# Weight halves off the second vector engine, and both input halves in one 512-column product, in a two-block transformer kernel

## The chip, the cores and the metric

One core of one Trainium2 chip runs the whole kernel in one launch. The metric is the device time of the launch in microseconds. Its engines are named as in the profile: PE (TensorE, matrix products; PEld is its weight loads), DVE (VectorE), ACT (ScalarE), POOL (GpSimd) and SP (SyncE, which here only issues the weight transfers). Each engine runs its own instructions in the order in which they were placed and waits on semaphores for the others.

## The reference

256 tokens of width 1024 go through two blocks, all in fp32. Cut to its skeleton:

```python
# block 1, layer 0 with MLA attention, layer 1 with NSA attention
x = layer_norm(a*x + 0.5*swiglu(x, ffn_w_gu[l,0], ffn_w_down[l,0]), ...)
x = layer_norm(a*x + concat(attention(x), memory_attention(...)) @ w_out[l], ...)
x = layer_norm(a*x + 0.5*swiglu(x, ffn_w_gu[l,1], ffn_w_down[l,1]), ...)

def swiglu(x, w_gu, w_down):              # w_gu 1024 x 5632, w_down 2816 x 1024
    g, u = split(x @ w_gu, 2)
    return (silu(g) * u) @ w_down

# block 2, layer 0: HGRN2 mixer, layer 1: RG-LRU mixer, each followed by PEER
h = rms_norm(x) * (1 + sc1) + sh1;  x = x + g1 * mixer(h)
h = rms_norm(x) * (1 + sc2) + sh2;  x = x + g2 * peer_ffn(h)

def peer_ffn(h, w_q, sub_keys, u_tab, v_tab):    # 16384 experts, 16 of them per head and token
    scores of 8 heads x 2 halves x 128 keys; top 16 of each half      # "first level"
    top 16 of the 16 x 16 sums: ids; gate = softmax(top_s)            # "second level"
    act = gelu(u_tab[ids] . h);  out = sum(gate * act * v_tab[ids])

# RG-LRU, one direction
r, ig = sigmoid(block_diag(xc, w_a) + b_a), sigmoid(block_diag(xc, w_x) + b_x)
log_a = -8 * r * softplus(-lam);  a = exp(log_a)
hs = linear scan of (a, sqrt(-expm1(2*log_a)) * ig * xc)
```

The vector of modulations (sc, sh, g) comes from a product of the condition with a large matrix ("ada"), which the kernel spreads over earlier stages.

## The kernel before, in words

**Split weights.** PE multiplies fp32 in a rounded form (fp32r). So each operand is kept as two halves, `hi` (rounded) and `lo` (what rounding left), and each product is taken three times: x_hi by w_hi, x_lo by w_hi, x_hi by w_lo. The weights come from memory as tiles of 128 x 1024 fp32 (512 KB each, one SP transfer, `wload`). `split` (L256) makes `hi` by an ACT copy (L262) and `lo` by a subtraction (L263). `lo_engine` (L247) says where the subtraction runs: `lo_pat` is a string cycled through, "V" for DVE and "P" for POOL. It is "VP" by default, so every second one is POOL's; after a norm the next `calm` (4 or 2) go to POOL whatever the pattern says. HGRN uses "PPV", the LRU "VPP" and "P", and the expert stages "V". `hi_pat` does the same for `hi` between ACT and DVE.

**linear** (L307) takes a weight tile of eight 128 x 128 pieces and streams the 256 tokens past it in three passes of eight products, 256 columns each: hi with XH, hi with XL, lo with XH. XH and XL are the two halves of the stage's input, two tiles. The feed-forward layers (`ffn`, L458) have 22 steps j, each of two tiles (gate and up) into the two halves of one PSUM bank, then a silu on ACT (L481), a multiply on DVE (L482) and the split of the result into AH and AL; then eight `down` products of 22 pieces each, with a residual sum. `stream(4, 3)` gives six places for a `hi` and its `lo`, so splits run some five tiles ahead. In each of 96 places one "fill" of the ada product runs on DVE (L966, L967). The first products after a norm (`begin`, `raws`) run on values that are not yet normalised.

**hgrn** (L1135) builds, per pair of heads, decayed queries and keys with many 128 x 256 DVE products (L1254, where one of the key products is POOL's). **lru** (L1446) has the gate loop (L1484 on: sigmoid, a DVE scaling at L1507, a tanh, a POOL product at L1510), an exponential (L1526), and scans (L1542). **peer** (L1565) multiplies by 16 wq tiles while DVE finds each first level (L1592 to L1596), and then takes 128 u tiles (`u_tile`) beside a list `todo` of smaller steps: 16 second levels, decodes, turns and gates. In the loop a `budget` grows by 1.7 a tile and a step is placed when the budget holds its cost. v tiles follow (`accumulate_tokens`, products of 512 columns at L1405 to L1407).

**What sets the order.** The order of each engine's instructions is fixed when the program is built, by a scheduler of the tile framework that goes by data dependences, the order in the code and a cost model. The pools limit how far a step may run ahead. PSUM has eight banks, four "mm" (matrix results of `linear`) and four "ax".

## Time and profile before

| | |
|---|---|
| median of 3 runs | 3166.89 us (3162.74 to 3168.49) |
| profiled execution | 3169.3 us, its span 3167.5 us |
| mean granted TensorE clock | 0.976 of full speed |
| PE busy | 3023.3 us, 95% of the span |
| DVE busy | 2360.8 us, 75% |
| ACT busy | 1656.8 us, 52% |
| POOL busy | 814.0 us, 26%, all but a little of it before 1412 us and between 2160 and 2400 us |

The stages, in us of the span: feed-forward 0 to 205, MLA to 350, feed-forward to 540 and (after a norm) to 765, NSA to 905, feed-forward to 1110, HGRN 1130 to 1345, expert searches to 1412, u tiles to 1800, v tiles to 2160, LRU to 2335, the second expert stage to the end. The rows are read as follows. "Busy" of PE includes time in which its pipeline is filled by overlapping products, so its pace is better read from the starts of successive groups of products. The mean duration of one instruction of a group, beside that of the same instruction at its fastest, shows whether it was held up while it ran. The chain of waits, followed back from the end, says which engine's work the end hung on.

### The profile page before, as it was taken

The page shows a single profiled execution, that of the slowest core. Times are in us where ns is not written, and L with a number is a line of the kernel's source. Part 1 is how long each engine was busy: PE and PEld are TensorE (multiplying, and loading weights), DVE is VectorE, ACT ScalarE, POOL GpSimd, SP SyncE. Part 2 cuts the span into 40 slices and gives each one's busy share as a digit, 9 for nine tenths or more (in the row PEclk, how much of TensorE's full clock was granted, in tenths as well). Part 3 has the DMA queues.
Part 4 walks back from the last instruction along what each step waited for, and adds up shares of the span by engine and source line. Part 5 has one row for each costly group of instructions (what it writes and reads, how often), then busy time and mean ns, then how long its engine had stood idle before and what let it go on. Part 6 is the DMA issues. An engine that isn't in the chain of part 4 may idle for free.

```text
span 3167.5 us, 57343 instructions
## 1 busy us (share of the span) xinstructions
PE 3023.3 (95%) x22268; PEld 2831.5 (89%) x22268; DVE 2360.8 (75%) x4441; ACT 1656.8 (52%) x2879; POOL 814.0 (26%) x393
## 2 busy tenths in 40 slices
PE   9999999999989979889999999998788999999998
PEld 8997999999789969889999988887788999988887
DVE  6866976964588598699888755558989888855555
ACT  5546554655554456546554555555545555455554
POOL 5643554755235345420000000003640000000000
PEclk9999999999999989999999999999899999999999
DMA  7852685885148433346444566665345544556664
GB/s 275 288 182 87 223 284 187 285 272 172 32 159 293 165 113 121 107 141 185 153 152 152 166 193 195 194 194 168 94 127 154 173 154 154 154 183 195 194 193 140
DMA packets 155794, 558.39 MB, mean 176 GB/s; under 512 B 17409, under 2 KB 19201, under 8 KB 155265
## 3 DMA queue, kind: packets, MB, share of 16 engines
q1 hardware_dynamic: 155232, 554.19, 54.1%
q8 instruction: 175, 2.87, 0.4%
q14 instruction: 99, 0.80, 0.1%
q10 hardware_dynamic: 288, 0.52, 0.0%
HBM read 553.60 MB, written 1.05 MB: 175 GB/s over the span
## 4 chain that ended last, share of the span: by engine, by line
PE 80%; DVE 14%; ACT 3%; issue 2%; DMA 1%; POOL 0%; DVEq 0%; ACTq 0%; SPq 0%; POOLq 0%
PE ps_mm L324 46%; PE ps_ax L1406 7%; PE ps_ax L1405 7%; PE ps_ax L1407 7%; PE ps_mm L1729 3%; DVE lo L263 2%; PE ps_mm L649 1%; PE ps_ax L324 1%; ACT hi L262 1%; DVE X L1051 1%; DVE RS L1113 1%; DVE M L1594 1%; PE ps_ax L540 1%; DVE M L1593 1%; DVE M L1596 1%
## 5 line engine op out<-in xcount | busy, mean ns | idle before, releaser
L262 ACT ACTIVATE hi<-raw 128x1024 fp32r<-128x1024 f32 (+1 forms) x948 | 987.4, 1048 | 868.8 <-PE ps_mm L324 382.8
L263 DVE TENSOR_TENSOR lo<-raw,hi 128x1024 fp32r<-128x1024 f32 (+2 forms) x698 | 919.6, 1319 | 530.7 <-ACT hi L262 519.3
L263 POOL TENSOR_TENSOR lo<-raw,hi 128x1024 fp32r<-128x1024 f32 (+2 forms) x261 | 663.7, 2549 | 1378.7 <-ACT hi L262 1326.8
L324 PE MATMUL ps_mm<-XH,hi 128*128 128x256 f32 (+1 forms) x4056 | 616.4, 290 | 26.8 <-ACT XH L1059 11.8
L324 PE MATMUL ps_mm<-XH,lo 128*128 128x256 f32 (+1 forms) x4056 | 587.5, 286 | 22.4 <-DVE lo L263 21.7
L324 PE MATMUL ps_mm<-XL,hi 128*128 128x256 f32 (+1 forms) x4056 | 585.1, 285 | 8.6 <-DVE XL L1060 5.6
L324 PEld LDWEIGHTS ps_mm<-XH,hi 128*128 128x128 f32 x4056 | 539.3, 192 | 35.4 <-ACT XH L1059 14.2
L324 PEld LDWEIGHTS ps_mm<-XH,lo 128*128 128x128 f32 x4056 | 535.2, 193 | 24.0 <-DVE lo L263 23.2
L324 PEld LDWEIGHTS ps_mm<-XL,hi 128*128 128x128 f32 x4056 | 532.0, 192 | 11.2 <-DVE XL L1060 7.7
L1407 PE MATMUL ps_ax<-lo,ah 128*128 128x512 f32 x1024 | 398.3, 389 | 0.0
L1406 PE MATMUL ps_ax<-hi,al 128*128 128x512 f32 x1024 | 398.3, 389 | 0.0
L1405 PE MATMUL ps_ax<-hi,ah 128*128 128x512 f32 x1024 | 398.3, 389 | 0.0
L1405 PEld LDWEIGHTS ps_ax<-hi,ah 128*128 128x128 f32 x1024 | 192.2, 188 | 40.1
L1407 PEld LDWEIGHTS ps_ax<-lo,ah 128*128 128x128 f32 x1024 | 192.2, 188 | 39.8
L1406 PEld LDWEIGHTS ps_ax<-hi,al 128*128 128x128 f32 x1024 | 192.2, 188 | 39.6
L1123 POOL TENSOR_SCALAR X<-X,VEC 128x256 f32<-128x256 f32 x4 | 3.7, 922 | 788.8 <-ACT RS L1109 786.8
L967 DVE SCALAR_TENSOR_TENSOR raw<-raw,one,cb 128x1024 f32<-128x1024 f32 x96 | 180.4, 1879 | 3.1 <-DMA raw<-in_ada_dram 0.2
L1736 ACT ACTIVATE M<-ps_mm 128x368 f32<-128x368 f32 (+42 forms) x128 | 43.8, 342 | 181.7 <-DVE M L1734 181.7
L1723 DVE TENSOR_TENSOR oh<-first,W 128x768 bf16<-128x768 bf16 x256 | 130.7, 550 | 0.0
L1729 PE MATMUL ps_mm<-oh 128*128 128x128 bf16 x1536 | 111.1, 220 | 0.0
L263 DVE TENSOR_TENSOR al<-M,ah 128x256 fp32r<-128x256 f32 x256 | 106.7, 418 | 1.2 <-ACT ah L262 1.2
L262 ACT ACTIVATE AH<-act 128x256 fp32r<-128x256 f32 x88 | 36.5, 417 | 133.4 <-DVE act L482 124.8
(457 smaller groups left out, 4044.2 us busy)
## 6 DMA issues: line engine op xcount, KB each, us to landing
raw<-in_pu_dram SPq DMA_DIRECT2D x256, 512.0 KB, 3.6
raw<-in_pv_dram SPq DMA_DIRECT2D x256, 512.0 KB, 3.5
raw<-in_gu_dram SPq DMA_DIRECT2D x175, 512.0 KB, 4.7
raw<-in_ada_dram SPq DMA_DIRECT2D x96, 512.0 KB, 4.5
raw<-in_down_dram SPq DMA_DIRECT2D x64, 512.0 KB, 4.4
raw<-in_hgin_dram SPq DMA_DIRECT2D x32, 512.0 KB, 3.6
raw<-in_wq_dram SPq DMA_DIRECT2D x32, 512.0 KB, 3.6
raw<-in_down_dram SPq DMA_DIRECT2D x32, 384.0 KB, 3.9
```

Of the source, the lines that this page charges most:

```text
L262: self.nc.scalar.activation(hi, src, AF.Copy)
L263: (eng or self.lo_engine()).tensor_tensor(lo, src, hi, op=ALU.subtract)
L324: mm(out, w[a][:, k], xin[b][:, k0 + k], start=k0 == 0 and at == 0, stop=k0 + n == kt and at == 3 * n - 1)
L540: nc.tensor.transpose(pt[:, bs], P[:, bs], self.ident)
L649: m(self.acc[b][:, k * T:k * T + T], w[:, 2 * b + k], x, start=t == 0 and w is hi and x is xh and k == 0, stop=t == KT - 1 and w is lo and ...
L967: nc.vector.scalar_tensor_tensor(w, w, tick, cb, op0=ALU.mult, op1=ALU.mult, accum_out=self.MOD[:, l, j:j + 1])
L1405: m(o, xh[:, ts], hi[:, cs], start=t == 0, stop=False)
L1406: m(o, xl[:, ts], hi[:, cs], start=False, stop=False)
L1407: m(o, xh[:, ts], lo[:, cs], start=False, stop=t == n - 1)
L1723: nc.vector.tensor_tensor(oh[:, q, 1:], first[:, q, None].to_broadcast([128, 3, 128, 2]), W3[:, :, None, t0 + 2 * q:t0 + 2 * q + 2].to_bro ...
L1729: nc.tensor.matmul(p[:, at:at + 128], oh[:, q, 0, :, t], oh[:, q, 1 + n, :, t], start=n == 0, stop=n == 2)
L1736: nc.scalar.activation(M[:, n:, ts], pv[:, n:], AF.Copy)
```

## The change

1. **lo.** `lo_pat` becomes "V" everywhere and `calm` goes. POOL keeps the subtraction only in `peer`: for most wq tiles, which a pattern "P" set inside `peer` (L1611) gives it before and now, and for u tiles that are placed while the next step of `todo` is a second level. There the budget grows by 2.4 a tile and a second level costs 2.4 (before 1.7 and 2.0), so one is placed per tile.
2. **Wide products.** XH and XL become the two halves of one tile XX, AH and AL of one tile AHL. `linear_wide` streams both at once: one product of 512 columns per piece of hi (x_hi into the bank's left half, x_lo into the right), then one of 256 columns per piece of lo into the left half. `fold` then adds the right half to the left: an ACT copy out of PSUM (L328) and a DVE add (L329). The feed-forward layers use it for gate and up, except for the first products after a norm, and for all `down` products. Each of gate and up now takes a bank of its own.
3. **HGRN** makes its last key product (28 instructions) on DVE. **LRU**: `hi` from "VA" and "V" to "A" and "VA"; the scaling at L1507 (16 instructions) is dropped, since tanh and exp now take a scale per channel, so that each of them runs 16 times on 256 columns where it ran 8 times on 512; the product at L1510 (8 instructions) goes from POOL to DVE.

```diff
@@ lo_engine
-        if self.calm:
-            self.calm -= 1
-            return self.nc.gpsimd
         e = self.lo_pat[self.lo_n % len(self.lo_pat)]
@@ new
+    def fold(self, p, t):
+        self.nc.scalar.activation(t, p[:, T:], AF.Copy)
+        self.nc.vector.tensor_tensor(p[:, :T], p[:, :T], t, op=ALU.add)
+
+    def linear_wide(self, p, wsrc, kt, xin, chunk=8):
+        mm = self.nc.tensor.matmul
+        for k0 in range(0, kt, chunk):
+            n = min(chunk, kt - k0)
+            hi, lo = self.first or self.wsplit(wsrc[:, k0:k0 + n, :], (n, 128))
+            self.first = None
+            for k in range(n):
+                mm(p.rearrange("p (a t) -> p a t", a=2), hi[:, k], xin[:, k0 + k], start=k0 + k == 0, stop=False,
+                   skip_group_check=True)
+            for k in range(n):
+                mm(p[:, :T], lo[:, k], xin[:, k0 + k, 0], start=False, stop=k0 + k == kt - 1, skip_group_check=True)
@@ ffn
+                        p = [self.ps(), self.ps()]
+                        for s in range(2):
+                            self.linear_wide(p[s], gu[li, j, s], KT, self.X2)
+                            self.fold(p[s], (sg, act)[s])
+                        nc.scalar.activation(sg, p[0][:, :T], AF.Silu)
+                        nc.vector.scalar_tensor_tensor(act, sg, 0.5, p[1][:, :T], op0=ALU.mult, op1=ALU.mult)
...
-                    self.linear(p[:, :T], self.A["down"][li, k], NF, (AH, AL))
+                    self.linear_wide(p, self.A["down"][li, k], NF, AHL)
+                    self.fold(p, pool.tile([128, T], F32, name="sg"))
@@ hgrn, lru
-                            (K[:, 1], K[:, 1], 1, eb[1][:, :, 0:1], nc.gpsimd)):
+                            (K[:, 1], K[:, 1], 1, eb[1][:, :, 0:1], nc.vector)):
...
-                                nc.vector.tensor_scalar(R[:, d, k], R[:, d, k], w[:, 4, c:c + 1], None, op0=ALU.mult)
+                                nc.scalar.activation(HS[:, d, k], R[:, d, k], AF.Tanh, scale=w[:, 4, c:c + 1])
-                    nc.scalar.activation(HS[:, d, k2], R[:, d, k2], AF.Tanh)
-                    nc.gpsimd.tensor_tensor(IG[:, d, k2], IG[:, d, k2], xc[:, k2], op=ALU.mult)
+                    nc.vector.tensor_tensor(IG[:, d, k2], IG[:, d, k2], xc[:, k2], op=ALU.mult)
@@ peer
-            second = [[(2.0, lambda h=h, a=a: second_level(h, a)) for h in range(8)] for a in range(2)]
+            second = [[(2.4, lambda h=h, a=a: second_level(h, a), "P") for h in range(8)] for a in range(2)]
...
-                budget += 1.7
+                side = todo[0][2:] if todo else ()
+                self.lo_pat = side[0] if side else "V"
+                budget += 2.4 if side else 1.7
```

What stands on the engines before and after, at three places (line numbers of the changed kernel are some 2 to 25 higher). **DVE in the first feed-forward layer's steps j**, before, two steps (`raw_…`, `cb` and `one` are the ada fill; every second step has the two `lo`):

```order
L482 SCALAR_TENSOR_TENSOR act_1387<-sg_1386,ps_mm_1388 128x256
L966 TENSOR_SCALAR one_1455<-act_1387 128x1
L967 SCALAR_TENSOR_TENSOR raw_1453,MOD_71<-raw_1453,one_1455,cb_614 128x1024
L263 TENSOR_TENSOR AL_145<-act_1387,AH_144 128x256
L482 SCALAR_TENSOR_TENSOR act_1459<-sg_1458,ps_mm_1460 128x256
L966 TENSOR_SCALAR one_1527<-act_1459 128x1
L967 SCALAR_TENSOR_TENSOR raw_1525,MOD_71<-raw_1525,one_1527,cb_614 128x1024
L263 TENSOR_TENSOR lo_1744<-raw_1741,hi_1743 128x1024
L263 TENSOR_TENSOR lo_1786<-raw_1783,hi_1785 128x1024
```

and now, one step:

```order
L329 TENSOR_TENSOR ps_mm_963<-ps_mm_963,sg_961 128x256
L260 TENSOR_TENSOR lo_1155<-raw_1152,hi_1154 128x1024
L260 TENSOR_TENSOR lo_1179<-raw_1176,hi_1178 128x1024
L329 TENSOR_TENSOR ps_mm_964<-ps_mm_964,act_962 128x256
L504 SCALAR_TENSOR_TENSOR act_962<-sg_961,ps_mm_964 128x256
L990 TENSOR_SCALAR one_1019<-act_962 128x1
L991 SCALAR_TENSOR_TENSOR raw_1017,MOD_70<-raw_1017,one_1019,cb_546 128x1024
L260 TENSOR_TENSOR AHL_143<-act_962,AHL_143 128x256
```

Each step has both its `lo` and both folds on DVE; the `lo` placed there belong to tiles some six ahead of the fold. **PE at the same place**, before, one step of two tiles:

```order
L324 MATMUL ps_mm_691<-XH_68,hi_694 128x256 x8
L324 MATMUL ps_mm_691<-XL_69,hi_694 128x256 x8
L324 MATMUL ps_mm_691<-XH_68,lo_695 128x256 x8
L324 MATMUL ps_mm_691<-XH_68,hi_724 128x256 x8
L324 MATMUL ps_mm_691<-XL_69,hi_724 128x256 x8
L324 MATMUL ps_mm_691<-XH_68,lo_725 128x256 x8
```

and now, a step and the beginning of the next:

```order
L340 MATMUL ps_mm_963<-XX_68,hi_967 128x512 x8
L343 MATMUL ps_mm_963<-XX_68,lo_968 128x256 x8
L340 MATMUL ps_mm_964<-XX_68,hi_991 128x512 x8
L343 MATMUL ps_mm_964<-XX_68,lo_992 128x256 x8
L340 MATMUL ps_mm_1024<-XX_68,hi_1028 128x512 x8
L343 MATMUL ps_mm_1024<-XX_68,lo_1029 128x256 x8
```

Two passes over the same hi have become one. **DVE at the start of the u tiles of the first expert stage** (first levels end at L1595 and L1596; L1629 to L1637 are second levels), before, with the `lo` of the first five u tiles:

```order
L263 TENSOR_TENSOR lo_16031<-raw_16028,hi_16030 128x1024
L1595 MAX M_15235<-M_15235 128x8
L263 TENSOR_TENSOR lo_16069<-raw_16066,hi_16068 128x1024
L1596 MAX_INDEX M_15235<-M_15235 128x8
L263 TENSOR_TENSOR lo_16107<-raw_16104,hi_16106 128x1024
L1637 MAX_INDEX M_15235<-M_15235 128x8
L1629 TENSOR_TENSOR M_15235<-M_15235 128x256 x2
L1633 MAX M_15235<-M_15235 128x8 x2
L1634 MAX_INDEX M_15235<-M_15235 128x8
L263 TENSOR_TENSOR lo_16145<-raw_16142,hi_16144 128x1024
L1635 MATCH_REPLACE M_15235<-M_15235 128x256
L263 TENSOR_TENSOR lo_16183<-raw_16180,hi_16182 128x1024
```

and now, around the first `lo` of a u tile that DVE has there, that of tile 9 (the first levels end some forty rows ahead of the first row):

```order
L1706 TENSOR_REDUCE gst_14541<-M_13783 128x8
L1661 MAX M_13783<-M_13783 128x8
L1707 RECIPROCAL gst_14541<-gst_14541 128x8
L1662 MAX_INDEX M_13783<-M_13783 128x8
L1708 TENSOR_TENSOR M_13783<-M_13783,gst_14541 128x128
L1698 TENSOR_TENSOR M_13783<-M_13783 128x2048
L1654 TENSOR_TENSOR M_13783<-M_13783 128x256
L1700 TENSOR_TENSOR M_13783<-M_13783 128x2048
L1658 MAX M_13783<-M_13783 128x8
L260 TENSOR_TENSOR lo_14892<-raw_14889,hi_14891 128x1024
L1702 TENSOR_TENSOR M_13783<-M_13783 128x8x128
L1659 MAX_INDEX M_13783<-M_13783 128x8
```

The `lo` of tiles 0 to 8 are POOL's now; that of tile 9 stands on DVE behind seven second levels and ten decode instructions.

## Rows read from the trace of the kernel before

**Rows 1.** The page: busy time by engine; the chain of waits by engine.

```profile
PE 3023.3 (95%) x22268; PEld 2831.5 (89%) x22268; DVE 2360.8 (75%) x4441; ACT 1656.8 (52%) x2879; POOL 814.0 (26%) x393
...
PE 80%; DVE 14%; ACT 3%; issue 2%; DMA 1%; POOL 0%; DVEq 0%; ACTq 0%; SPq 0%; POOLq 0%
```

**Rows 2.** Stretches: width, busy us (count) of PE, PEld, DVE, ACT, POOL; clock.

```profile
13.00:121.00 108.00, 107.83 (x892) 107.75 (x892) 86.17 (x112) 60.66 (x87) 65.99 (x29) 0.98 0.81 280
...
205.00:350.00 145.00, 134.70 (x938) 119.33 (x937) 104.63 (x242) 94.62 (x204) 53.45 (x27) 0.98 0.35 120
...
1130.00:1345.00 215.00, 192.78 (x1413) 183.27 (x1413) 171.06 (x293) 130.47 (x272) 111.18 (x66) 0.94 0.35 111
...
2160.00:2260.00 100.00, 82.97 (x592) 80.49 (x591) 95.60 (x134) 59.91 (x109) 61.33 (x30) 0.88 0.44 147
2260.00:2335.00 75.00, 49.17 (x330) 46.60 (x329) 67.89 (x107) 29.78 (x56) 32.63 (x13) 0.82 0.27 86
```

**Rows 3.** Timeline of PE, feed-forward: start us, us, products (x8 a pass).

```profile
100.67 1.12 PE L324 MATMUL ps_mm<-XH,hi 128*128 128x256 f32 x8
...
110.21 1.12 PE L324 MATMUL ps_mm<-XL,hi 128*128 128x256 f32 x8
```

**Rows 4.** Timeline of PE, v tiles of the first expert stage, 512 columns.

```profile
1812.17 0.39 PE L1405 MATMUL ps_ax<-hi,ah 128*128 128x512 f32 x1
...
1818.29 0.39 PE L1405 MATMUL ps_ax<-hi,ah 128*128 128x512 f32 x1
```

**Rows 5.** Groups of DVE, 1500 to 1780 us (POOL idle): busy us, mean ns.

```profile
L263 DVE TENSOR_TENSOR lo<-raw,hi 128x1024 fp32r<-128x1024 f32 x81 | 99.2, 1225 | 35.7 <-ACT hi L262 32.7 <-ACT M L1744 1.7
```

**Rows 6.** Groups, feed-forward, 13 to 121 us, DVE and ACT.

```profile
L482 DVE SCALAR_TENSOR_TENSOR act<-sg,ps_mm 128x256 f32<-128x256 f32 x17 | 7.0, 411 | 0.1
...
L481 ACT ACTIVATE sg<-ps_mm 128x256 f32<-128x256 f32 x18 | 6.6, 366 | 0.0
```

**Rows 7.** DVE by line, whole span: ns of one, min/median/max.

```profile
L1051 DVE SCALAR_TENSOR_TENSOR X<-X,VEC,RS x24: 470/472/2642, 336.6 to 916.5; 128x256 f32<-128x256 f32 x24
...
L967 DVE SCALAR_TENSOR_TENSOR raw<-raw,one,cb x96: 1272/1289/3422, 66.7 to 1057.0; 128x1024 f32<-128x1024 f32 x96
...
L1254 DVE TENSOR_TENSOR Q<-Q,E x48: 400/416/2612, 1152.6 to 1275.8; 128x256 f32<-128x256 f32 x48
...
L1507 DVE TENSOR_SCALAR R<-R,spw x16: 334/581/2459, 2206.8 to 2238.6; 128x256 f32<-128x256 f32 x16
```

**Rows 8.** DVE group of L1051, whole span: busy us, mean ns.

```profile
L1051 DVE SCALAR_TENSOR_TENSOR X<-X,VEC,RS 128x256 f32<-128x256 f32 x24 | 22.9, 1022 | 0.0
```

**Rows 9.** MLA, 205 to 350 us: chain of waits by line, then DVE lo.

```profile
by line: PE ps_mm L649 12.5%; DVE lo L263 8.2%; ACT hi L262 5.9%; DVE X L1051 5.1%; PE ps_ax L776 5.1%; issue 4.5%; PE ps_ax L769 4.5%; PE ps_ax L540 3.9%; DVE RS L381 3.6%; DVE qt L670 3.2%; PE ps_ax L410 2.7%; ACT XH L447 2.3%; PE ps_ax L
...
L263 DVE TENSOR_TENSOR lo<-raw,hi 128x1024 fp32r<-128x1024 f32 x11 | 20.3, 1843 | 3.5 <-ACT hi L262 3.3
```

**Rows 10.** HGRN, 1130 to 1345 us: groups of DVE and of POOL.

```profile
L1254 DVE TENSOR_TENSOR Q<-Q,E 128x256 f32<-128x256 f32 x48 | 30.0, 654 | 0.0
...
L263 POOL TENSOR_TENSOR lo<-raw,hi 128x1024 fp32r<-128x1024 f32 x32 | 81.7, 2557 | 69.7 <-ACT hi L262 67.0 <-PE ps_mm L324 1.6 <-DVE K L1254 1.1
```

**Rows 11.** LRU, 2160 to 2335 us: groups of DVE and of POOL.

```profile
L263 DVE TENSOR_TENSOR lo<-raw,hi 128x1024 fp32r<-128x1024 f32 x9 | 21.2, 2359 | 1.3 <-ACT hi L262 1.1
...
L1507 DVE TENSOR_SCALAR R<-R,spw 128x256 f32<-128x256 f32 x16 | 14.3, 927 | 1.2 <-ACT R L1502 1.2
...
L263 POOL TENSOR_TENSOR lo<-raw,hi 128x1024 fp32r<-128x1024 f32 x29 | 74.6, 2585 | 67.1 <-ACT hi L262 50.7 <-issue 4.6 <-ACT late L1463 4.0
```

**Rows 12.** Timeline of PE at the first u tiles of both expert stages.

```profile
1384.62 1.11 PE L324 MATMUL ps_mm<-XH,hi 128*128 128x256 f32 x8
...
1400.78 5.49 PE L324 MATMUL ps_mm<-XH,lo 128*128 128x256 f32 x24 [10.26 <-DVE lo L263]
...
2391.09 5.43 PE L324 MATMUL ps_mm<-XH,lo 128*128 128x256 f32 x24 [8.03 <-DVE lo L263]
```

**Rows 13.** Groups of DVE, 1412 to 1500 us, POOL idle.

```profile
L1634 DVE FIND_INDEX8 M<-M 128x8 uint32<-128x256 f32 x10 | 4.2, 420 | 0.0
```

More of the change, by code (lines that the diff above doesn't have):

```diff
@@ L184, in __init__ @@
         self.seq_n = {"raw": 0, "hi": 0}
-        self.lo_pat = "VP"
+        self.lo_pat = "V"
         self.fills = deque()
@@ L189, in __init__ @@
         self.shift = None
-        self.calm = 0
         self.raws = deque()
@@ L207, in input_tiles @@
     def input_tiles(self):
-        self.XHc, self.XLc = (self.cp.tile([128, KT, T + 2], F32R, name=n, tag=n) for n in ("XH", "XL"))
+        self.XX = self.cp.tile([128, KT, 2, T + 2], F32R, name="XX", tag="XX")
+        self.XHc, self.XLc = self.XX[:, :, 0], self.XX[:, :, 1]
         self.XH, self.XL = self.XHc[:, :, :T], self.XLc[:, :, :T]
+        self.X2 = self.XX[:, :, :, :T]
     def constants(self, phases, bp):
@@ L442, in layer_norm @@
         self.fresh = True
-        self.calm = 4
         for k in range(KT):
@@ L461, in ffn @@
         with self.stream(4, 3), tc.tile_pool(name="ffn", bufs=2) as pool:
-            AH = pool.tile([128, NF, T], F32R, name="AH", bufs=1)
-            AL = pool.tile([128, NF, T], F32R, name="AL", bufs=1)
+            AHL = pool.tile([128, NF, 2, T], F32R, name="AHL", bufs=1)
+            AH, AL = AHL[:, :, 0], AHL[:, :, 1]
             gu = self.A["gu"]
@@ L622, in mix_start @@
         self.ob = self.ps("ax", 3)
-        self.zp = [self.cp.tile([128, 4, 512], F32, name=n, tag=t) for n, t in (("z", "XH"), ("P", "XL"))]
+        zp = self.cp.tile([128, 2 * KT * (T + 2)], F32, name="zp", tag="XX")
+        self.zp = [zp[:, 2048 * i:2048 * i + 2048].rearrange("p (a b) -> p a b", b=512) for i in range(2)]
         self.count = {"score": 0, "mixed": 0, "out": 0, "softmax": 0}
@@ L1027, in begin @@
         self.fresh = "banks"
-        self.calm = 2
         for n, src in enumerate(srcs):
@@ L1319, in hgrn @@
             self.rms_sum(pool)
-            self.lo_pat = "VP"
+            self.lo_pat = "V"
     def prepare(self):
@@ L1341, in prepare @@
         lam = self.vec("lru_lam_2", 0, 16)
-        w = self.sp = self.cp.tile([128, 5, 16], F32, name="spw")
+        w = self.sp = self.cp.tile([128, 6, 16], F32, name="spw")
         nc.scalar.activation(w[:, 0], lam, AF.Abs)
@@ L1486, in lru @@
                 if b:
-                    self.hi_pat = "VA"
-                    self.lo_pat = "VPP"
+                    self.hi_pat = "A"
+                    self.lo_pat = "V"
                 for d in range(2):
@@ L1513, in lru @@
             YB = pool.tile([128, KT], F32, name="YB")
-            self.hi_pat = "V"
-            self.lo_pat = "VPP"
+            self.hi_pat = "VA"
+            self.lo_pat = "V"
             self.hi_n = self.lo_n = 0
@@ L1525, in lru @@
                 for d in range(2):
-                    nc.scalar.activation(R[:, d, ks], R[:, d, ks], AF.Exp, scale=-2.0, bias=late[:, 0:1])
+                    for k in (2 * i, 2 * i + 1):
+                        nc.scalar.activation(R[:, d, k], R[:, d, k], AF.Exp, scale=w[:, 5, 8 * d + k:8 * d + k + 1],
+                                             bias=late[:, 0:1])
                     nc.vector.scalar_tensor_tensor(IG[:, d, ks], R[:, d, ks], 1.0, IG[:, d, ks],
@@ L1550, in lru @@
             self.hi_pat = "A"
-            self.lo_pat = "P"
+            self.lo_pat = "V"
             self.sqrt_soon(pool, Y[:, KT - 1, 0:1])
@@ L1562, in lru @@
             self.rms_sum(pool)
-            self.lo_pat = "VP"
+            self.lo_pat = "V"
     def peer(self, l):
@@ L1787, in peer @@
                 self.rms_sum(vpool)
-            self.lo_pat = "VP"
+            self.lo_pat = "V"
     def final(self):
```

9 lines of the change are left out of this document (5 added, 4 removed).

## The prediction

> **What bounds the kernel now.** I read the page first. PE is busy 95% of the span, DVE 75%, POOL 26%, and the chain of waits lies 80% on PE and 14% on DVE [rows 1]. That is an average over stages with different limits, so next the busy time by stretch. In the feed-forward layers (13 to 121 us) PE is busy 107.8 of 108 us: there only PE's pace counts, and DVE has 22 us of room. In MLA, HGRN and LRU PE has gaps, and in the LRU DVE is busy 163.5 of 175 us [rows 2]: there DVE's time counts.
>
> Third, how long a DVE instruction takes. The same L1051 instruction takes 0.470 us at its fastest and 2.642 at its slowest, and L1254, L967 and L1507 spread as widely [rows 7]. A `lo` on DVE takes 1.225 us where POOL is idle [rows 5], 1.843 in MLA [rows 9] and 2.359 in the LRU [rows 11], while POOL has `lo` of its own of about 2.57 us [rows 10, 11]. The slowest times are about a free instruction and most of one POOL instruction: DVE waits inside the instruction for POOL. So the change has three effects: a better PE pace in the feed-forward layers, freed DVE time elsewhere, and more work on DVE, namely POOL's.
>
> **Wide products.** Ten passes of eight 256-column products span 9.54 us, 119.3 ns each [rows 3]; 27 products of 512 columns span 6.12 us, 226.7 ns each [rows 4]. One wide product for two narrow ones saves 238.5 - 226.7 = 11.8 ns. The order has 152 wide tiles of gate and up (8 products each) and 32 `down` sums (22 each): 1216 + 704 = 1920, all in stretches that PE bounds. Term: **-22.7 us**.
>
> The Trainium skill ("TensorE: Matmul & The Clock Gate", "Back-to-back issue gap") gives an isolated warm product N/2.4 ns plus about 2.5, so a pair would save only those 2.5 ns, 4.8 us in all as an estimate. The trace's 119.3 ns for 256 columns is above its 109, and its 226.7 above its 216, so the rows decide.
>
> The price is a fold per tile. Its ACT copy is like L481 (0.366 us), its DVE add, with one operand in PSUM, like L482 (0.411, not slowed beside POOL) [rows 6]. A step j has 16 wide and 16 narrow products, 16 x (226.7 + 119.3) = 5.53 us of PE. DVE has in it two `lo` (2.45), two adds (0.82), L482 (0.41), AL (about 0.41, as L1254's 128 x 256 product) and, in most steps, a fill (1.27): 5.37 us, some 0.3 less where records overlap. That leaves hardly 5% but is below PE's time, and `lo` run some six tiles ahead, so a late fold delays nobody at once. I cost steady state at nothing; the cover is thin, and the first rival is its loss. At the end of each layer the last fold lies on the path: 0.37 + 0.41 = 0.8 us, four times. Term: **+3.2**.
>
> **Norms and transitions around the feed-forward layers.** L1051 takes 24 x (1.022 - 0.470) = 13 us more than at its fastest [rows 7, 8], at the head of MLA and in two transitions. Summing mean less fastest over the DVE pieces on the chain in the transitions between 350 and 1130 us gives about 25 us in all. Against it, some ten `lo` there (the `calm` ones) now stand on DVE in front of or between these, 10 x 1.225 = 12. Term: **-13**, between -25 and +3 (every `lo` exposed at both its own cost and a wait).
>
> **MLA.** Of the 145 us the chain has 8.2% on DVE `lo` (11.9 us), 5.1% on L1051 (7.4) and 3.2% on L670 (4.6) [rows 9]. At free durations these would be 11.9 x 1.225/1.843 = 7.9, 8 x 0.47 = 3.8 and (for three of L670's, of L1051's kind) 3 x 0.47 = 1.4: 10.8 us less, and the smaller pieces bring it to about 16. Eighteen `lo` come to DVE, 22 us, of which the chain's share of DVE's time (about 40 of 105 us) is 8. Term: **-8**. NSA has little POOL contention on its chain: **+1**.
>
> **HGRN.** The 48 L1254 products cost 48 x (0.654 - 0.400) = 12.2 us over their fastest [rows 7, 10]; the same over all DVE groups of the stage gives some 53. To DVE come 32 `lo` (39 us), 28 key products (11.5) and 6 small splits (2.5): 53. So DVE's 171 us [rows 2] stay. What changes is the chain, which has DVE on it for about 67 us: 22 of the excess lie on it and 6 of POOL's key products, and 53 x 67/171 = 21 come back. Term: **-7**, between -25 (all new `lo` beside other work) and +20 (half of them ahead of what PE waits for).
>
> **LRU.** Here DVE is full. Removed: 9 x (2.359 - 1.225) = 10.2 us on its `lo`, L1507's whole 14.3 us [rows 11], and about 42 of excess on some ten other kinds by the same rule, less 15 that stay because the next stage's wq `lo` remain on POOL; some seven `hi` casts that go to ACT, 4. Together 55. Added: 20 `lo` (29 on POOL less the wq ones [rows 11]), 24.5; eight products from POOL, about 0.68 each, 5.4; small splits, 2. Together 32. Net -23, of which DVE's 163.5/175 counts, and ACT's sixteen small exps for eight large ones cost a little: **-19**, between -30 and -5.
>
> **Expert stages.** PE stands 10.3 us at 1390.5 and 8.0 at 2383 for the first u tile's `lo` on DVE, behind the first levels, and the next 24 products take 5.5 us instead of 2.86 [rows 12]: 23.5 us lost in all. Now POOL makes that `lo` (about 2.57 us a tile against PE's 2.86), so PE goes on. But the `lo` of tile 9 is DVE's, behind seven second levels (six instructions of 0.42 us each [rows 13], some 2.2 where they overlap) and ten decode steps, of which a few are done earlier, so DVE reaches it some 18 us after its first levels end at 1400: at 1418 to 1419. PE began tile 0 at 1384.62 and wants that pass at 1384.6 + 9 x 2.86 + 1.9 = 1412.3. It stands 7 us again, with its slow start. What is late next is tile 9: the stall moves. Saved: 3 a stage, **-6**; between -23 and +4.
>
> **Sum.** -22.7 + 3.2 - 13 - 8 + 1 - 7 - 19 - 6 = -71.5, on the profiled execution's 3169.3: 3097.8. That execution is 2.4 above the median, so **3095**.
>
> **Rivals.** (a) *DVE becomes the bound of the feed-forward steps.* For: 5.37 against 5.53 us, and in each step two folds wait for PE's last product and ACT's copy; if DVE stands 0.4 us at each with its next `lo` queued behind, a step takes 6.2 us, more than the 5.72 (48 x 119.3 ns) of before. It begins at 5.53, has eaten these steps' gain at 5.72 (76 steps x 0.19 = 14.4 us) and makes the kernel slower from about 6.1. At 6.2, 76 steps x 0.67 = +51 on the sum; a DVE that full also leaves the transitions, MLA and HGRN nothing (+28): 3095 + 79 = 3174, slower. Against: the fills are in most steps, not all, and the six tiles of lead carry single waits. (b) *The freed DVE time buys nothing where PE or ACT bounds*, the moved `lo` filling it whole: MLA, transitions, HGRN and experts at nothing, LRU at half: 3095 + 13 + 8 + 7 + 6 + 10 = 3139. (c) *The wide product doesn't pay*, its second half being read from another stretch of the tile and the weight load still the pace: 3095 + 23 = 3118. By the Trainium skill's rule above (same section) it would be 3113. (d) *The stalls vanish*: u tiles keep going because tile 9's `lo` meets a faster DVE, and HGRN hides its `lo`: 3095 - 17 - 18 = 3060. That the change doesn't do what it says is ruled out by the order: POOL keeps few instructions.
>
> **Chances.** Forecast (3075 to 3115) 0.42; (d) 0.16; (c) 0.10; (b) 0.17; (a) 0.15. This kernel's measurement tells about 0.2% (6 us) from no change. Cases (d), forecast, (c) and nearly all of (b) are faster: 0.83; the upper edge of (b) and the lower of (a) within 0.2%: 0.05; the rest of (a) slower: 0.12. The range reaches from (d) with its bounds, 3040, to most of the way to (a), 3165, leaving out about 0.17.
>
> **What would show it.** Right: wide products at 227 ns and narrow ones at 119 without gaps in the feed-forward steps; L1051's successor at 0.47 us everywhere before 1300; a `lo` on DVE at 1.23 except beside the wq tiles; PE waiting for DVE `lo` near tile 9 of each u stage, not at tile 0; the LRU some 19 us shorter. Wrong: PE idle behind `lo` or folds in the feed-forward steps, or HGRN longer than 215 us, which would mean that POOL's help was worth more than the contention it caused.

## The result: 74.7 us less, by another sum than the one forecast

| | before | after |
|---|---|---|
| median (runs) | 3165.81 us (4) | 3091.12 us (4; 3088.99 to 3097.02) |
| profiled span | 3167.5 us | 3095.1 us |
| ratio, 95% interval | | 0.9767 (0.975 to 0.9785) |

The page of the changed kernel, answering to [rows 1]: busy time by engine and the chain of waits.

```profile
PE 2994.4 (97%) x20348; PEld 2719.4 (88%) x20348; DVE 2392.2 (77%) x4900; ACT 1719.6 (56%) x3088; POOL 202.6 (7%) x100
...
PE 82%; DVE 11%; ACT 4%; DMA 2%; issue 1%; POOL 0%; DVEq 0%; SPq 0%; ACTq 0%
```

DVE has 459 instructions more and is busy only 31 us longer. The instruction that [rows 7, 8] followed (L1051, now L1074; min/median/max ns) is never held up any more where it writes X, as in the row below. Where the same line writes M, at the head of the expert stages, one beside a wq `lo` on POOL still takes 2.695 us. A `lo` in the LRU takes what one took beside an idle POOL [rows 5]:

```profile
L1074 DVE SCALAR_TENSOR_TENSOR X<-X,VEC,RS x24: 471/477/480, 328.7 to 888.5; 128x256 f32<-128x256 f32 x24
```

```profile
L260 DVE TENSOR_TENSOR lo<-raw,hi 128x1024 fp32r<-128x1024 f32 x31 | 37.7, 1221 | 0.5 <-ACT hi L259 0.5
```

The stages, in us, cut in both traces at the starts of the same instructions (L445, L1051, L1133 and L1405 of before):

| stage | before | after | change | forecast |
|---|---|---|---|---|
| four feed-forward layers, with the norms between them | 846.1 | 822.7 | -23.4 | -32.5 |
| MLA | 123.3 | 118.1 | -5.2 | -8 |
| NSA | 142.1 | 142.3 | +0.2 | +1 |
| norm ahead of HGRN, HGRN | 201.0 | 184.2 | -16.8 | -7 |
| LRU | 141.0 | 108.8 | -32.2 | -19 |
| u tiles and searches, both stages | 956.1 | 959.6 | +3.5 | -6 |
| all others | 757.9 | 759.4 | +1.5 | 0 |

So the total (-72.4 by the spans) is what was forecast, but the feed-forward layers and the expert stages gave 18.6 us less than expected and HGRN and the LRU 23 more. The experiments go through these four.

**Feed-forward.** PE stays the bound; answering to [rows 2], 13 to 121 us, with no POOL:

```profile
13.00:121.00 108.00, 108.00 (x625) 95.64 (x624) 98.07 (x188) 72.20 (x126) 0.00 (x0) 1.00 0.88 300
```

Its timeline (start us, us, products), one tile and then the same place eleven tiles after the first row, answering to [rows 3]:

```profile
86.23 1.11 PE L343 MATMUL ps_mm<-XX,lo 128*128 128x256 f32 x8
87.17 2.02 PE L340 MATMUL ps_mm<-XX,hi 128*128 128x512 f32 x8
89.03 1.10 PE L343 MATMUL ps_mm<-XX,lo 128*128 128x256 f32 x8
...
116.99 1.10 PE L343 MATMUL ps_mm<-XX,lo 128*128 128x256 f32 x8
```

30.76 us for eleven tiles is 2.796 us a tile against 24 x 119.3 ns = 2.863 before: 0.067 saved, where 8 x 11.8 ns = 0.094 was forecast. Eight wide products take 1.86 us from their start to that of the narrow ones behind them, 232 ns each, not the 226.7 of [rows 4].

**Expert stages.** What PE waited for from 1290 to 1450 us (total us, times, longest), and ACT from 1340 to 1450:

```profile
PE ps_mm L321 <- ACT hi L259: 11.1, 1, 11.1
PE ps_mm L321 <- DVE lo L260: 3.1, 1, 3.1
```

```profile
ACT M L1694 <- DVE M L1684: 13.3, 2, 10.6
```

PE's stand left the first u tile, as forecast, and came back some nine tiles on, but not behind DVE's `lo`: ACT's copy for the decode (L1694) waited 10.6 us for DVE, with the `hi` of the next u tiles queued behind it. The stand costs more than its length: behind it the granted clock is at its lower level (1.2 GHz, 0.51 of full speed in the stretch below), and sixteen products take 3.78 us instead of 2.06.

```profile
1365.00:1379.00 14.00, 5.72 (x27) 5.72 (x28) 14.00 (x40) 10.25 (x12) 4.75 (x2) 0.51 0.11 39
```

### The profile page after: what moved, and what is told of

Its sections match the earlier page's. It is cut to its first block, busy times and chain, and to the rows that moved or that the text cites. A ratio compares the mean times of both kernels' runs of the same rounds, so it can differ in the third digit from the quotient of the medians.

```text
span 3095.1 us, 53666 instructions
## 1 busy us (share of the span) xinstructions
PE 2994.4 (97%) x20348; PEld 2719.4 (88%) x20348; DVE 2392.2 (77%) x4900; ACT 1719.6 (56%) x3088; POOL 202.6 (7%) x100
## 4 chain that ended last, share of the span: by engine, by line
PE 82%; DVE 11%; ACT 4%; DMA 2%; issue 1%; POOL 0%; DVEq 0%; SPq 0%; ACTq 0%
PE ps_mm L321 26%; PE ps_mm L340 13%; PE ps_ax L1431 8%; PE ps_ax L1430 7%; PE ps_ax L1429 7%; PE ps_mm L343 7%; PE ps_mm L1754 3%; PE ps_ax L321 2%; PE ps_mm L673 1%; DMA raw<-in_gu_dram 1%; DVE lo L260 1%; ACT hi L259 1%; PE ps_ax L1265 1%; DVE M L1654 1%; DVE M L1619 1%
## 5 line engine op out<-in xcount | busy, mean ns | idle before, releaser
L260 DVE TENSOR_TENSOR lo<-raw,hi 128x1024 fp32r<-128x1024 f32 (+2 forms) x893 | 1077.5, 1209 | 531.7 <-ACT hi L259 523.4
L321 PE MATMUL ps_mm<-XX,hi 128*128 128x256 f32 (+1 forms) x5680 | 793.9, 290 | 40.3 <-ACT hi L259 26.4
L321 PEld LDWEIGHTS ps_mm<-XX,hi 128*128 128x128 f32 x5680 | 726.8, 193 | 50.9 <-ACT hi L259 27.7
L321 PE MATMUL ps_mm<-XX,lo 128*128 128x256 f32 (+1 forms) x2840 | 411.9, 285 | 6.0 <-DVE lo L260 6.0
L321 PEld LDWEIGHTS ps_mm<-XX,lo 128*128 128x128 f32 x2840 | 374.2, 193 | 7.4 <-DVE lo L260 7.3
L340 PE MATMUL ps_mm<-XX,hi 128*128 128x512 f32 x1216 | 310.4, 396 | 4.8 <-ACT sg L503 4.5
L340 PEld LDWEIGHTS ps_mm<-XX,hi 128*128 128x128 f32 x1216 | 219.0, 189 | 45.9 <-ACT sg L503 6.4
L260 POOL TENSOR_TENSOR lo<-raw,hi 128x1024 fp32r<-128x1024 f32 x66 | 169.3, 2571 | 1363.1 <-ACT hi L259 1345.8
L343 PEld LDWEIGHTS ps_mm<-XX,lo 128*128 128x128 f32 x1216 | 164.6, 189 | 16.2 <-DVE lo L260 3.5
L340 PE MATMUL ps_mm<-AHL,hi 128*128 128x512 f32 x704 | 177.7, 393 | 0.0
L343 PE MATMUL ps_mm<-XX,lo 128*128 128x256 f32 x1216 | 169.3, 282 | 0.9 <-DVE lo L260 0.7
L340 PEld LDWEIGHTS ps_mm<-AHL,hi 128*128 128x128 f32 x704 | 125.8, 188 | 21.7
```

Of the source, the lines that this page charges most:

```text
L260: (eng or self.lo_engine()).tensor_tensor(lo, src, hi, op=ALU.subtract)
L321: mm(out, w[a][:, k], xin[b][:, k0 + k], start=k0 == 0 and at == 0, stop=k0 + n == kt and at == 3 * n - 1)
L340: mm(p.rearrange("p (a t) -> p a t", a=2), hi[:, k], xin[:, k0 + k], start=k0 + k == 0, stop=False, skip_group_check=True)
L343: mm(p[:, :T], lo[:, k], xin[:, k0 + k, 0], start=False, stop=k0 + k == kt - 1, skip_group_check=True)
```

## The experiments

Each run has runs of the kernel before beside it, whose medians lie between 3167.0 and 3169.7 us; the ratios are to those.

### The wide products alone

```diff
 # before, with XX, AHL, linear_wide and fold in the feed-forward layers;
 # every weight half stays where it was
...
+                            self.linear_wide(p[s], gu[li, j, s], KT, self.X2)
+                            self.fold(p[s], (sg, act)[s])
```

> The kernel before with the wide products alone; every weight half stays where it was. Theory A (PE sets the pace of these layers and the wide product is worth what the changed kernel's timeline shows): a gate/up tile takes 2.80 us instead of 2.86 and a down sum 7.66 instead of 7.87, so 152 x 0.066 + 32 x 0.21 = 17 us saved, less 3 for four folds at the layers' ends: 14 us faster, about 3152, nearly all in the four feed-forward layers. Theory B (without freeing DVE from GpSimd the folds don't fit): a fold's add waits behind weight halves that take 1.6 us and more beside GpSimd, PE stands, and the kernel is within 5 us of the one before or slower.

Measured: 3211.43 us, ratio to before 1.0133 (1.0118 to 1.0149): 44 us *slower*. A timeline of DVE in the first feed-forward layer shows how:

```profile
64.55 2.61 DVE L265 TENSOR_TENSOR AHL<-act,AHL 128x256 fp32r<-128x256 f32 x1
67.08 0.42 DVE L334 TENSOR_TENSOR ps_mm<-ps_mm,sg 128x256 f32<-128x256 f32 x1
...
69.72 3.04 DVE L997 SCALAR_TENSOR_TENSOR raw<-raw,one,cb 128x1024 f32<-128x1024 f32 x1
...
72.69 0.42 DVE L334 TENSOR_TENSOR ps_mm<-ps_mm,sg 128x256 f32<-128x256 f32 x1
```

and the waits of PE in front of wide products, over the whole span, say what that costs:

```profile
PE ps_mm L345 <- POOL AHL L265: 13.4, 3, 4.8
...
PE ps_mm L345 <- ACT sg L509: 10.0, 8, 2.6
...
PE ps_mm L345 <- DVE act L510: 6.9, 11, 1.0
```

The fold (L334) is not slow (0.42 us), but it stands in order behind a small split that POOL holds up to 2.61 us and a fill held up to 3.04. Until the fold is done the silu can't run, and until the silu (`sg`) and the multiply (`act`) have read the bank, PE can't begin the tile that uses it next: those are the last two rows. The first lies in the first `down` sum of a layer, at its last pieces, where PE waits for the last step's small split at the end of the same chain. PE is busy 102.0 of the 108 us where it was 107.8. Theory B, and the mechanism of rival (a), with its price: the four layers are 11.4 us longer each on average.

### The change without the wide products

```diff
 # after, with linear (three passes of 256 columns) in the feed-forward layers, no fold
-                            self.linear_wide(p[s], gu[li, j, s], KT, self.X2)
+                            self.linear(p[:, s * T:(s + 1) * T], gu[li, j, s], KT, self.xin)
```

> The changed kernel with the narrow products of before in the feed-forward layers (no 512 columns, no folds), all else changed. Theory A: the wide products' part is 14 us, so this one is at about 3105. Theory B (the fold's price on DVE or at the layers' ends eats the better pace): at 3091 or below. Theory C (the full 22.7 us of the prediction, hidden by another loss): at 3111 or above.

Measured: 3100.19 us (ratio 0.9787), between theories A and B. So on top of the other parts the wide products are worth 9.1 us by the medians, a gain that isn't quite clear of the noise (0.9774 to 0.9801 without them, 0.975 to 0.9785 with them), and on their own they cost 44: what the edit is worth depends on whether POOL shares DVE's time. By the two profiled executions (spans 3100.9 and 3095.1) the feed-forward layers take 823.6 us without and 822.7 with them, although PE's pace is better: what the pace gives, new stands take. The longest of them in the changed kernel (timeline of PE, the wait in brackets):

```profile
552.80 2.50 PE L340 MATMUL ps_mm<-XX,hi 128*128 128x512 f32 x5 [2.71 <-ACT sg L503]
```

```profile
917.91 1.66 PE L340 MATMUL ps_mm<-XX,hi 128*128 128x512 f32 x6 [1.65 <-ACT sg L503]
```

```profile
1067.45 0.70 PE L426 MATMUL ps_ax<-X,ONED 128*128 128x256 f32 x2 [2.09 <-DVE X L408]
```

The first two are the bank held by the silu behind a fold, as in the run before, at the first wide steps after a norm, where DVE has much to do (6.3 and 7.2 us in the 8 us up to them); the third is the last fold of a layer, in front of the norm, and behind it the granted clock is 0.51 for 7 us, where it stays at 1.00 with narrow products. The rest of the 9.1 lies in no single stage (2.3 in the LRU, 1.0 in MLA), where no product is wide; the runs of each kernel spread by 8 us, and where it comes from stays open.

### The LRU's part alone

```diff
 # before, with the LRU's hunks
-                    self.hi_pat = "VA"
-                    self.lo_pat = "VPP"
+                    self.hi_pat = "A"
+                    self.lo_pat = "V"
...
-                                nc.vector.tensor_scalar(R[:, d, k], R[:, d, k], w[:, 4, c:c + 1], None, op0=ALU.mult)
+                                nc.scalar.activation(HS[:, d, k], R[:, d, k], AF.Tanh, scale=w[:, 4, c:c + 1])
...
```

> The kernel before with only the LRU's part: its weight halves on DVE, the scaling folded into tanh and exp, the product off GpSimd. Theory A (DVE is full there and everything that leaves it counts): the stage shrinks by the 32 us that it lost in the changed kernel, 141 to 109 us, kernel at about 3134. Theory B (the prediction's -19 is right and the rest came with the stages around it): 3147.

Measured: 3140.2 us (0.9911; 0.9896 to 0.9926), 27 us less, between the two theories. The stage itself takes 118.9 us, 22 less than before, and 10 more than in the changed kernel, where POOL has left its first tiles too (one instruction there instead of eight). The stretch in before, here and in the changed kernel (width, busy PE, PEld, DVE, ACT, POOL, granted clock):

```profile
2161.10:2302.10 141.00, 107.21 (x747) 103.92 (x746) 132.01 (x193) 72.76 (x132) 79.08 (x36) 0.84 0.37 121
```

```profile
2156.50:2275.40 118.90, 99.15 (x746) 96.57 (x745) 104.63 (x196) 84.14 (x157) 20.85 (x8) 0.90 0.41 135
```

```profile
2118.90:2227.70 108.80, 95.56 (x747) 93.14 (x746) 102.05 (x203) 84.55 (x157) 7.77 (x1) 0.94 0.43 146
```

From the first to the last DVE has ten instructions more and 30.0 us less to do, and the stage is 32.2 us shorter. PE's busy time falls too, by 11.7 us for the same products: it stands less, and the granted clock of the stretch goes from 0.84 to 0.94.

### POOL's work put back, for nobody

```diff
 # after; in the LRU, for two of three weight tiles
+                dmy = self.twin.tile([128, 1024], BF16, name="dmy", tag="dmy", bufs=1)
+                self.nc.gpsimd.tensor_tensor(self.shaped(dmy, shape), raw, hi, op=ALU.subtract)
```

> The changed kernel with 15 more GpSimd instructions in the LRU: two of three weight halves there are computed a second time on GpSimd into a tile that nobody reads; DVE does all its work as in the changed kernel. Theory A (GpSimd holds up DVE's instructions with two SBUF inputs; no work is moved, only the hold-up comes back): the DVE means rise as in the kernel before, the stage grows by 15 x 1 to 2 us, kernel at 3106 to 3121. Theory B (the stage gained by what was taken out or sped up, scaling, product and shorter weight halves, not by the missing hold-up): within 4 us of 3091.

Measured: 3118.95 us (0.9849), 27.8 us more than the changed kernel. In the LRU (width 136.3 instead of 108.8):

```profile
2111.30:2247.60 136.30, 102.99 (x747) 99.46 (x746) 131.50 (x202) 84.77 (x157) 49.10 (x16) 0.86 0.36 121
```

```profile
L262 DVE TENSOR_TENSOR lo<-raw,hi 128x1024 fp32r<-128x1024 f32 x31 | 46.0, 1488 | 0.0
L1575 DVE TENSOR_TENSOR_SCAN HS<-R,IG 128x256 f32<-128x256 f32 x16 | 16.6, 1074 | 0.0
...
L1541 DVE TENSOR_TENSOR IG<-IG,xc 128x512 f32<-128x512 f32 x8 | 12.1, 1507 | 2.1 <-ACT IG L1534 2.1
```

```profile
L302 POOL TENSOR_TENSOR dmy<-raw,hi 128x1024 bf16<-128x1024 f32 x15 | 46.3, 3086 | 780.5 <-DVE lo L262 721.6 <-ACT hi L261 23.4 <-issue 16.2
```

The same DVE instructions take 29.4 us longer (131.5 against 102.05), though no DVE work was added; the scans went from 0.678 to 1.074 us, the 128 x 512 products from 0.689 to 1.507. That is 2 us of DVE for each POOL instruction, whose result nobody waits for. Theory A. The extra instructions also keep a weight tile's buffers until they are done, which this run doesn't separate, but a wait for a buffer stands in front of an instruction and isn't counted in its duration.

### HGRN's part alone

```diff
 # before, with these two
-                            (K[:, 1], K[:, 1], 1, eb[1][:, :, 0:1], nc.gpsimd)):
+                            (K[:, 1], K[:, 1], 1, eb[1][:, :, 0:1], nc.vector)):
...
-            self.lo_pat = "PPV"
+            self.lo_pat = "V"
```

> The kernel before with only HGRN's part: weight halves on DVE and the last key product on DVE. Theory A (GpSimd's instructions held DVE's up, and that was dearer than the work that GpSimd took): the stage goes from 186 to some 174 us as in the changed kernel, the kernel to about 3154. Theory B (the stage's gain comes from its first weights or norm, so from the default pattern): within 4 us of the kernel before.

Measured: 3150.22 us (0.9943; 0.9929 to 0.9957), 17 us less: theory A. The stage before, in the changed kernel and in this run:

```profile
1126.50:1312.50 186.00, 168.57 (x1246) 161.09 (x1247) 146.54 (x252) 116.60 (x247) 96.68 (x61) 0.94 0.34 105
```

```profile
1093.40:1267.30 173.90, 164.88 (x1246) 158.00 (x1247) 146.80 (x314) 116.99 (x247) 2.79 (x2) 0.95 0.36 122
```

```profile
1120.40:1292.80 172.40, 164.84 (x1246) 158.14 (x1247) 145.58 (x313) 116.68 (x247) 2.74 (x2) 0.97 0.38 120
```

As worked out, DVE's busy time in the changed kernel is the same to 0.3 us: what came from POOL (62 instructions) is just what the hold-up had cost. The stage is 12 us shorter all the same. By the chain of waits DVE's time no longer lies on the path: added up by engine, the chain through the stage has 102.7 us of PE, 54.9 of DVE, 11.2 of ACT and 5.7 of POOL in the kernel before; in this run it has 152.5 of PE, 13.2 of DVE, 5.7 of ACT and none of POOL. Whether the held-up DVE instructions or POOL's own time (2.6 us for a `lo` that takes DVE 1.2) put DVE on the path, no run shows apart. Alone, this part brings the stage from 186.0 to 172.4 us and the norm ahead of it from 15.0 to 10.3.

### The default pattern alone

```diff
 # before
-        self.lo_pat = "VP"
+        self.lo_pat = "V"
 # and without calm; HGRN, LRU, expert loop and products as before
```

> The kernel before with the default pattern 'V' and no calm count: the weight halves of the feed-forward layers, MLA and NSA on DVE, narrow products, HGRN, LRU and expert loop as before. Theory A (DVE's freed waits at the norms and in MLA count on their own): the stages of the first block gave 33 us in the changed kernel, 9 of which are the wide products' by the kernel with narrow ones, so about -24, 3143. Theory B (they are hidden by PE and come only together with the rest): within 6 us of the kernel before.

Measured: 3148.85 us (0.9947; 0.9934 to 0.9961), 18 us less. By its trace the feed-forward layers lose 23.5 us and MLA 5.1; the norm ahead of HGRN takes 16.6 us instead of 15.0 and the LRU 144.5 instead of 141.0, and the rest is spread. Nearer theory A: 29 us for 24 in its own stages, of which the whole kernel keeps 18. And the feed-forward layers' whole gain in the changed kernel (23.4) is there without one wide product. The longest of their stretches, before and here:

```profile
336.60:765.30 428.70, 418.07 (x3468) 413.52 (x3467) 323.44 (x423) 222.46 (x325) 241.84 (x104) 0.98 0.73 248
```

```profile
329.60:746.00 416.40, 412.55 (x3470) 408.53 (x3470) 325.24 (x525) 224.09 (x325) 1.01 (x2) 1.00 0.77 253
```

PE stands 3.9 us instead of 10.6, and is busy 5.5 us less for the same products, with a granted clock of 1.00 instead of 0.98. Over all four layers it stands 13.6 us less and is busy 9.9 us less.

### The expert loop, four ways

The loop of before on the changed kernel:

```diff
-            second = [[(2.4, lambda h=h, a=a: second_level(h, a), "P") for h in range(8)] for a in range(2)]
+            second = [[(2.0, lambda h=h, a=a: second_level(h, a)) for h in range(8)] for a in range(2)]
...
-                self.lo_pat = side[0] if side else "V"
-                budget += 2.4 if side else 1.7
+                budget += 1.7
```

> The changed kernel with the expert loop of before (u tiles' weight halves on DVE, budget 1.7 a tile). Theory A (the loop's change only moves PE's stand from the first u tile to about the ninth, where ACT's copy of hi stands behind a decode step): its part is about +3.5 us over both stages, by the two stages' lengths before and after (477.2 to 480.1 and 478.9 to 479.5), so this kernel is at about 3088. Theory B (the prediction: 3 us a stage are saved): at 3097.

Measured: 3083.04 us (0.9733), 8 us *less* than the changed kernel: its loop costs 8 us. That is theory A's direction, with more than twice its size. PE waits in the second expert stage, with this loop and (second fence) with the changed one:

```profile
PE ps_mm L321 <- DVE lo L260: 8.6, 2, 8.1
```

```profile
PE ps_mm L321 <- ACT hi L259: 10.2, 1, 10.2
PE ps_mm L321 <- DVE lo L260: 2.9, 1, 2.9
```

One stand of 8.1 us at the first u tile became one of 10.2 and one of 2.9. Then a loop in which ACT's decode copies can't come early (shown in part; the copies take the bias too, and the order of `todo` changes so that the first of them comes after u tile 12):

```diff
+                    nc.scalar.activation(zt, M[:, done[0] - 1, 0:1], AF.Copy, scale=0.0)
+                    nc.scalar.activation(w, w, AF.Exp, bias=zt)
...
-                self.lo_pat = side[0] if side else "V"
+                self.lo_pat = "P" if i < 24 else "V"
```

> The changed kernel with another expert loop: the first 24 u tiles' weight halves on GpSimd, and the two decode steps that ACT takes (spread copies, exponential) tied by a bias to the u tile emitted last, so that they can't stand in ACT's queue ahead of the hi of earlier tiles; the first of them comes after u tile 12, not 6. Theory A (PE's stand of 11.1 us at 1362 us, and its slow start, came from hi copies queued behind a spread copy that waited for DVE): the stand goes, some 10 to 14 us a stage, kernel at 3065 to 3075. Theory B (the stand is DVE's total work after the first levels, and moves on again, to the first weight half that DVE has): 3091 within 5.

Measured: 3097.4 us (0.9776), 6 us more than the changed kernel. ACT's wait is gone, and PE stands for something else in the first stage:

```profile
PE ps_ax L1726 <- DVE M L1706: 15.7, 1, 15.7
```

These are the transposes of `turn`, which stand on PE ahead of u tiles that are ready. Theory B in its first half: the lateness is DVE's, and whoever is next in its way stands. So the transposes were moved back (shown in part, against the changed kernel; the second half of `todo` moves too):

```diff
-            todo.extend(second[0] + first[:4] + second[1][:2] + first[4:] + second[1][2:4] + turns[:1] + second[1][4:])
+            todo.extend(second[0] + first[:1] + second[1] + [(1.7, lambda: None)] + first[1:] + turns[:1])
```

> Third form of the expert loop, on the changed kernel: as in the run before with 24 u tiles' weight halves on GpSimd and ACT's decode copies tied to the u tile emitted last, but all sixteen second levels come first, the first copies are tied to u tile 18, and the transposes of the first turn stand on PE behind u tiles 19 and 22, the second turn some nine tiles after. Theory A (DVE trails its place in the order by some 16 us when the first levels end, and whoever waits for it first stands; let it catch up behind work that needs no DVE, and nobody does): no stand of PE over 4 us between the first levels and the gates, kernel at 3068 to 3078. Theory B (GpSimd's halves slow DVE and DVE never catches up): a stand of 8 us or more, at 3085 or above.

Measured: 3079.38 us (0.9723). PE's stand in the first stage (the second stage has 2.5):

```profile
PE ps_ax L1726 <- DVE M L1706: 12.5, 1, 12.5
```

Neither theory as written: the second stage is mended and the first not, where DVE still comes 12.5 us late. The same with a pause of 8.5 instead of 1.7, four tiles later:

```diff
-            todo.extend(second[0] + first[:1] + second[1] + [(1.7, lambda: None)] + first[1:] + turns[:1])
+            todo.extend(second[0] + first[:1] + second[1] + [(8.5, lambda: None)] + first[1:] + turns[:1])
```

> The run with the tied expert loop, and its first turn four tiles (11.4 us) later still; nothing else. In that run PE stood 12.5 us at the first turn's transposes in the first expert stage and 2.5 in the second. Theory A (DVE is 12 us late there and early enough four tiles on): the stand goes to under 2 us, kernel at 3066 to 3071. Theory B (the gates end that much later and the last u tiles then wait for them, or the stand moves to the first weight halves of DVE): within 4 us of 3079 or slower.

Measured: 3060.66 us (0.9662; 0.9649 to 0.9675). The longest waits of PE in the first stage are now

```profile
PE ps_ax L1069 <- DVE RS L1136: 4.5, 1, 4.5
PE ps_mm L321 <- ACT hi L259: 1.7, 2, 1.2
```

of which the first is the norm's. Each expert stage, v tiles included, takes 811.6 us, against 826.1 and 827.9 before and 829.1 and 828.5 in the changed kernel. The stand is as theory A had it, and the time 5 us below its range: 30 us better than the changed kernel. Part of that is the clock. The same stretch of the span in the changed kernel and here, where PE hardly stands:

```profile
1345.00:1430.00 85.00, 70.78 (x552) 70.37 (x552) 78.52 (x240) 42.62 (x57) 30.27 (x12) 0.88 0.40 135
```

```profile
1345.00:1430.00 85.00, 84.48 (x712) 84.25 (x712) 79.63 (x220) 49.32 (x68) 46.96 (x20) 1.00 0.56 182
```

What the 24 halves on POOL contribute to this loop, no run shows by itself.

### Two on the pace of the wide products

The products of a tile in turns, wide and narrow, with the loop of before:

```diff
             for k in range(n):
                 mm(p.rearrange("p (a t) -> p a t", a=2), hi[:, k], xin[:, k0 + k], ...)
-            for k in range(n):
                 mm(p[:, :T], lo[:, k], xin[:, k0 + k, 0], ...)
```

> The changed kernel with the expert loop of before (as in the run at 3083) and with the two kinds of products of a tile alternating: 512 columns with a piece of hi, then 256 with the same piece of lo. Theory A (a wide product takes 232 ns and not 227 because of where its columns come from, or of other traffic): a tile stays at 2.80 us, kernel at 3083 within 4. Theory B (it is the weight load of a run of wide products): the tile's time changes by 0.1 us or more, 152 tiles and 32 sums together by over 20 us, either way. PE then also needs a tile's lo 1.6 us earlier, which the splits' lead of six tiles covers.

Measured: 3096.05 us (0.9773), 13 us slower than the run with that loop. A pair of starts, from its timeline:

```profile
84.15 0.39 PE L340 MATMUL ps_mm<-XX,hi 128*128 128x512 f32 x1
84.38 0.28 PE L342 MATMUL ps_mm<-XX,lo 128*128 128x256 f32 x1
...
88.36 0.40 PE L340 MATMUL ps_mm<-XX,hi 128*128 128x512 f32 x1
```

Twelve pairs in 4.21 us, 351 ns a pair, hardly more than in the changed kernel (2.796/8 = 349.5): the order of the weight loads is not what makes a wide product 232 ns. The time bound of theory A failed nevertheless: the feed-forward layers take 832.6 us instead of 819.8. About half of that is pace after all: over the four layers the median pair takes 352 ns instead of 350 in gate and up, and 353 instead of 347 in `down`, 6.6 us for 1216 and 704 pairs. Another 5 us are stands: the lead of the splits doesn't cover the earlier `lo`. In the second and third layer (328.8 to 749.8 us) PE has this wait, the longest 3.2 us:

```profile
PE ps_mm L342 <- DVE lo L260: 5.4, 2, 3.2
```

What sets 232 against 227 stays open.

And the fastest kernel with narrow `down` products:

```diff
-                    self.linear_wide(p, self.A["down"][li, k], NF, AHL)
-                    self.fold(p, pool.tile([128, T], F32, name="sg"))
+                    self.linear(p[:, :T], self.A["down"][li, k], NF, (AH, AL))
```

> The same kernel with the down products narrow again, in three passes and without their folds; gate and up stay wide. Theory A (the prediction: 32 x 22 x 11.8 ns = 8.3 us of the gain are theirs, less 3 for the folds at the layers' ends): 5 us slower than the run beside it. Theory B (the traces: a narrow down product took 117.0 ns before, a wide one takes 229.8 and its narrow neighbour 117.8, so a wide pair saves 3.4 ns, 2.4 us in all, which the four folds on the path eat): within 3 us of the run beside it, or faster.

Measured: 3060.59 us (0.9657), beside 3060.66 with wide ones. Theory B: the half of the edit that the forecast valued at 8 us is worth nothing in this kernel.

## Why the prediction came out, point by point

- **Wide products, -22.7 + 3.2.** Mis-sized, twice. The first step that failed is taking 226.7 ns from the v tiles and 119.3 from gate and up for all 1920 pairs. Gate and up ran at 232 wide and saved 0.067 us a tile, 10.2 us for 152. The `down` sums had been faster than 119.3 ns a product already (117.0). The same place of a sum in the timelines of PE, seven sums apart before, and six after:

```profile
141.64 1.10 PE L324 MATMUL ps_mm<-AL,hi 128*128 128x256 f32 x8
...
195.72 1.12 PE L324 MATMUL ps_mm<-AL,hi 128*128 128x256 f32 x8
```

```profile
137.53 2.00 PE L340 MATMUL ps_mm<-AHL,hi 128*128 128x512 f32 x8
...
183.42 2.00 PE L340 MATMUL ps_mm<-AHL,hi 128*128 128x512 f32 x8
```

  7.73 us a sum against 7.65: 0.08 x 32 = 2.5 us, where 8.3 was forecast. The pace thus gives 12.7 us. The second is the steady state "at nothing": the cover held there (PE busy 108.0 of 108 us), but not at the first wide steps after a norm, where banks wait for folds. In the profiled executions that leaves the layers about 1 us; the three longest stands are 6.5 us of what is missing, and where the rest lies stays open. The medians say 9.1 for the whole kernel.
- **Transitions and MLA, -13 and -8.** With the default pattern alone, 23.5 and 5.1 us. Right in kind; the transitions were under-sized by 10 us, so that the feed-forward layers' total (-23.4) is theirs and not the wide products'. The term counted DVE's pieces on the chain, and PE's standing did fall by about that, 13.6 us. It had nothing for the 9.9 us by which PE is also busy less for the same products, at a granted clock of 1.00 where the stretches had 0.97 to 0.99 before.
- **HGRN, -7.** DVE's balance came out to 0.3 us. What was mis-sized is the 21 us that "come back": the term put DVE's new work on the chain at DVE's old share of it, 67 of 171 us. In the run with this part alone the chain has 13.2 us of DVE where it had 54.9, and the stage with its norm came out 10 us shorter than forecast.
- **LRU, -19.** The mechanism was shown by the run that put POOL's work back (+28 us for work that nobody needs). The term was under-sized by its reserve for hold-up that stays: the stage's own stretch has none of it left, and DVE's work fell by 30 us, not 23. And of its 23 the term let only 19 count, where 30.0 us of DVE became 32.2 of the stage.
- **Expert stages, -6.** The stall moved to about the ninth tile, as forecast, and DVE began its first u-tile `lo` 17 us after the first levels ended (1356.9 to 1373.8), where 18 were forecast. The step that failed is "POOL makes that `lo`, so PE goes on": it looked at DVE's queue alone. ACT's queue holds the decode copies ahead of the `hi` of the same tiles, so PE stood longer than before. Both stages together take 3.5 us more than before, and 8 us more than with the loop of before, instead of saving 6.
- **Rival (a)** was the right one to fear. It did not decide here because POOL left; with POOL in place it is 44 us slower than before. Rival (b) fell with the run of the default pattern, rival (c) was half right: the pace gives 12.7 of its 22.7 us, and in the products' own layers next to nothing of that is left. Of (d) HGRN gave 10 of its 18 us beyond the forecast, and the expert stages theirs only in the last loop.

The total was right because the terms erred in both directions: 9 us too much in the feed-forward layers and 9.5 in the expert stages, 10 too little in HGRN and 13 in the LRU. Nothing in the working makes these errors cancel. That DVE would gain by POOL's leaving was understood; that the sum came out within 4 us is luck.
